# Weights and modulation weights loaded in halves of a unit

## The chip, the cores and the metric

The kernel runs on one core of one Trainium2 chip. The metric is the device time of one execution in microseconds, as a median of runs. TensorE (PE) does the matrix products, VectorE (DVE) and ScalarE (ACT) the elementwise work, GpSimd (POOL) a few fills, and SyncE (SP) issues the DMAs.

## The reference

One sequence of 256 tokens with 1024 channels goes through seven stages in fp32. Before each of the first four stages the input is normalised and modulated by a shift and a scale, and the result is gated; these factors come from a condition vector of 1024 numbers:

```
mod = silu(c) @ ada_w[layer] + ada_b[layer]   # 1024 -> 6*1024, two layers
h = rmsnorm(x) * (1 + scale) + shift
x = x + gate * rmsnorm(mixer(h));  x = x + gate2 * rmsnorm(mlp(h2))
```

The stages are a mixer of a state space scan and neighbourhood attention (mixer0), an MLP of 4096 (mlp0), a chunked mLSTM (mixer1), a second MLP (mlp1), a mixer of three branches (mixer2: softmax attention with a forget gate, a diagonal state space, a gated linear recurrence), a cross attention on 256 memory tokens (cross), and a gated feed-forward of 2816 (ffn). All weights, 214 units of 1 MB, and 48 MB of modulation weights are read from DRAM once.

## The kernel before, in words

The tokens stand transposed in SBUF as a high and a low part (`xh`, `xl`), rounded values and remainders; a weight is split in the same way, and a product is three matmuls (high by high, high by low, low by high).

A **unit** is 1 MB of weights, 128 partitions by 2048 numbers, contiguous in DRAM (`prepare` packs them so). `unit` (line 433) takes a raw buffer of 8 KB a partition out of the pool `raw` (`RAW_BUFS = 3`), issues one DMA on SP (line 440), and then works by halves of 1024 columns: ScalarE writes the rounded high part `wh` (line 450, instruction at L353), VectorE the remainder `wl` (line 451, L362). The cast halves have pools of their own, `wh` and `wl`, with `W_BUFS = 4` buffers each, so two units. In phases that have room some units go to further buffers (`fwh`, `fwl`; `extra`). The users of units are `proj_tok` and `proj_feat` (a projection of 256 outputs: 48 matmuls of 256 columns; both of its output parts run over all eight 128-row slices, so the first half of the unit is needed until three quarters of it, the second to the end), `proj_half`, and `down` (24 matmuls of 512 columns).

The **modulation weights** use the same raw buffers. `first_norm` (line 610) loads the eight units for the first shift and scale at the start (`load`, line 632); VectorE reduces each half against the condition row in one instruction (L640). `ada` (line 732) does the rest in the background of mixer0, mlp0, mixer1 and mlp1, one unit a step: one DMA (line 749) and two VectorE instructions (L753 for shift and scale, L358 and L365 for gates).

The order of the work is not written by hand. The program is traced in the order of the code; `tick` interleaves side work and background steps with the projections by credits. A planner then gives each engine its instructions by priority (the order of the trace) with its own estimates of time, and lets an instruction take a buffer when it expects it to be free. Casts are raised by `CAST_FIRST = 120` places, but `held` keeps them behind the end of the norm between two stages. On the chip each engine runs its list in order; a DMA on SP that waits for its buffer holds all later DMAs, since every load and store of the kernel is issued there.

Of the kernel before, what the change touches and what calls it, by code (L numbers as in the profile page):

```python
# [11 lines left out]
F32 = mybir.dt.float32  # L12
# [7 lines left out]
P = 128  # L20
D = 1024
T = 256
NEG = -1.0e30
NOSYNC = mybir.DependencyInfo(mybir.DependencyClass.NoSync, mybir.DependencyReason.DATA)
RAW_BUFS = 3
W_BUFS = 4
NB_BUFS = 4

CAST_FIRST = 120
# [94 lines left out]
def prepare(i):  # L124
# [40 lines left out]
    for l in range(2):  # L165
        for ch in range(6):
            part = aw[l, :, ch] if ch % 3 == 2 else aw[l, :, ch].T
            ada.append(part.reshape(4, 2, P, D).transpose(0, 2, 1, 3).reshape(4, P, 2048))
    ada = np.concatenate(ada, 0)

    sm = np.zeros((P, N_WSM), f)
# [84 lines left out]
    for gg in range(2):  # L256
        blk[gg, :, :, :, gg, :] = c5[:, :, gg].transpose(3, 0, 1, 2)
    c5 = blk.reshape(P, 2 * 16 * 32)
    return {
        "x": i["x"][0], "mem": i["mem_2"][0], "wts": wts, "ada": ada, "wsm": sm, "cols": cols,  # L260
        "rows": rows, "cst": cst, "hgm": hgm, "tvec": tvec, "nab": nab.reshape(16, P, 512),
        "b5": b5, "c5": c5,
# [8 lines left out]
class Stack:  # L271
    def __init__(self, ctx, tc, aps):
        self.tc, self.nc, self.a = tc, tc.nc, aps
        pool = lambda name, bufs, **kw: ctx.enter_context(tc.tile_pool(name=name, bufs=bufs, **kw))
        self.const = pool("const", 1)
        self.raw_p = pool("raw", RAW_BUFS)
        self.wh_p = pool("wh", W_BUFS)
        self.wl_p = pool("wl", W_BUFS)
        self.xT_p = pool("xT", 1)
# [150 lines left out]
            self.tick(1)  # L430


    def unit(self, u, n, extra=False):
        if self.early > 0:
            extra, self.early = True, self.early - 1
        free = False
        if not extra and self.free > 0:
            free, self.free = True, self.free - 1
        raw = self.raw_p.tile([P, 2048], F32, tag="raw", name="raw")
        self.nc.sync.dma_start(out=raw, in_=self.a["wts"][u])  # L440
        hi, lo = [], []
        for i in range(2):
            src = raw[:, i * 1024:(i + 1) * 1024]
            if extra:
                h, l = self.pt("fwh", [P, 1024], F32R, 4), self.pt("fwl", [P, 1024], F32R, 4)
            else:
                h = self.wh_p.tile([P, 1024], F32R, tag="wh", name="wh")
                l = self.wl_p.tile([P, 1024], F32R, tag="wl", name="wl")
            with self.held(not extra and not free), self.tc.high_priority(CAST_FIRST):
                self.act(h, src)  # L450
                self.tt(l, src, h, ALU.subtract)
            hi.append(h.rearrange("p (k n) -> p k n", n=n))
            lo.append(l.rearrange("p (k n) -> p k n", n=n))
        m = 1024 // n
        return [(hi[k // m][:, k % m], lo[k // m][:, k % m]) for k in range(2048 // n)]
# [154 lines left out]
    def first_norm(self):  # L610


        nc = self.nc
        self.mod[0] = self.const.tile([P, 2, 2, 8], F32, tag="mod0", name="mod0")
        mod = self.mod[0][:, 0]
        self.xh, self.xl = self.new_xT()
        tps = []

        def transposed():
            tps.extend(self.ax((P, 2, T)) for _ in range(4))  # L620
            for t in range(2):
                xn = self.xn([P, D])
                r = self.rms(self.x[t], xn)
                for g in range(2):
                    gs = slice(g * 512, (g + 1) * 512)
                    self.act(xn[:, gs], self.x[t][:, gs], scale=r[:, 0:1])
                    for k in range(4 * g, 4 * g + 4):
                        self.transpose(tps[k // 2][:, k % 2, t * P:(t + 1) * P], xn[:, k * P:(k + 1) * P])

        sums = []  # L630

        def load(u):
            s8 = self.sm(4, "fns", bufs=4)
            sums.append(s8)
            for what in range(2):
                raw = self.raw_p.tile([P, 2048], F32, tag="raw", name="raw")
                nc.sync.dma_start(out=raw, in_=self.a["ada"][what * 4 + u])
                acc = self.pt("acc", [P, D])
                for k in range(2):
                    nc.vector.tensor_tensor_reduce(out=acc, in0=raw[:, k * D:(k + 1) * D], in1=self.crow, scale=1.0, scalar=0.0,  # L640
                                                   op0=ALU.mult, op1=ALU.add, accum_out=s8[:, 2 * what + k:2 * what + k + 1])

        load(0)
        yield
        transposed()
        for u in range(4):
            us = slice(2 * u, 2 * u + 2)
            s8 = sums[u]
            bcol = lambda what: self.col("adab", what * 8 + 2 * u, 2)
            self.tt(mod[:, 1, us], s8[:, 0:2], bcol(0), ALU.add)  # L650
            self.tt(s8[:, 2:4], s8[:, 2:4], bcol(1), ALU.add)
            self.stt(mod[:, 0, us], s8[:, 2:4], 1.0, self.col("ng", 2 * u, 2), ALU.add, ALU.mult)
            f = self.pt("bp", [P, 2, T], bufs=2)
            for k in range(2):
                kk = 2 * u + k
                a1, b1 = mod[:, 0, kk:kk + 1], mod[:, 1, kk:kk + 1]
                self.act(f[:, k], tps[u][:, k], AF.Identity, scale=a1, bias=b1)
            self.act(self.xh[:, us], f)
            self.tt(self.xl[:, us], f, self.xh[:, us], ALU.subtract)
            if u < 3:  # L660
                load(u + 1)
            yield
# [69 lines left out]
    def ada(self, layer, chunks, G=None, kind="ax"):  # L732

        nc = self.nc
        if self.mod[layer] is None:
            self.mod[layer] = self.const.tile([P, 2, 2, 8], F32, tag=f"mod{layer}", name=f"mod{layer}")
        mod = self.mod[layer]
        for ch in chunks:
            half, what = ch // 3, ch % 3
            acc = self.pt("acc", [P, D])  # L740
            s8 = self.sm(8, "ads")
            rows = []
            for i in range(4 if what == 2 else 0):
                cs = slice(i // 2 * 512, (i // 2 + 1) * 512)
                rows.append(self.pt("grow", [P, 512], F32, 2))
                nc.sync.dma_start(out=rows[-1], in_=self.a["rows"][4 * (i % 2) + layer * 2 + half, cs].partition_broadcast(P))
            for u in range(4):
                raw = self.raw_p.tile([P, 2048], F32, tag="raw", name="raw")
                nc.sync.dma_start(out=raw, in_=self.a["ada"][(layer * 6 + ch) * 4 + u])
                for k in range(2):  # L750
                    w, j = raw[:, k * D:(k + 1) * D], 2 * u + k
                    if what != 2:
                        nc.vector.tensor_tensor_reduce(out=acc, in0=w, in1=self.crow, scale=1.0, scalar=0.0,  # L753
                                                       op0=ALU.mult, op1=ALU.add, accum_out=s8[:, j:j + 1])
                    elif j == 0:
                        self.ts(acc, w, self.cond[:, 0:1], None, ALU.mult)
                    else:
                        self.stt(acc, w, self.cond[:, j:j + 1], acc, ALU.mult, ALU.add)
                yield
            if what == 2:  # L760
                for c in range(2):
                    cs = slice(c * 512, (c + 1) * 512)
                    pb = self.ps(kind)
                    self.matmul(pb, self.ones[:, 0:P], acc[:, cs])
                    self.tt(G[:, cs], pb, rows[2 * c], ALU.add)
                    self.tt(G[:, cs], G[:, cs], rows[2 * c + 1], ALU.mult)
            else:
                bcol = self.col("adab", (layer * 4 + half * 2 + what) * 8, 8)
                if what == 0:
                    self.tt(mod[:, half, 1], s8, bcol, ALU.add)  # L770
                else:
                    self.tt(s8, s8, bcol, ALU.add)
                    self.stt(mod[:, half, 0], s8, 1.0, self.col("ng", (layer * 2 + half) * 8, 8),
                             ALU.add, ALU.mult)
            yield
# [1191 lines left out]
```

## Time and profile before

| | us |
|---|---|
| median of 3 runs | 1510.37 (1508.34 to 1513.8) |
| the profiled execution | 1509.47 |
| its span, first to last instruction | 1507.7 |
| PE busy in it | 1429.2 |
| VectorE busy | 1156.5 |
| ScalarE busy | 864.2 |

The profiled execution has a granted TensorE clock of 0.992 of full speed in the mean. The span is what the rows below are measured in; 1.8 us lie around it. A busy PE is one with a matmul under way: matmuls overlap, so a single one lasts longer than the distance to the next. A wait names who waited and who ended it; a wait of an engine that is not the slowest costs nothing by itself.

### The profile page before, as it was taken

What the parts mean: (1) busy time and instruction counts of PE and PEld (TensorE: products, weight loads), DVE (VectorE), ACT (ScalarE), POOL (GpSimd) and SP (SyncE); (2) the same over time, 40 slices, a digit from 0 to 9 for tenths busy, and PEclk for the clock granted to TensorE, in tenths of its full rate; (3) what the DMA queues carried; (4) which work ended last, traced back from release to release, by engine and by line L of the source; (5) the groups of instructions that cost most, each with busy time, mean ns of one, the idle gap of its engine ahead of it and who ended that gap; (6) DMA issues with size and microseconds to landing.
All of it is one profiled execution on the core that took longest, in us unless ns stands there. A gap on an engine that the chain in (4) does not pass through costs nothing.

```text
span 1507.7 us, 25356 instructions
## 1 busy us (share of the span) xinstructions
PE 1429.2 (95%) x9932; PEld 1299.5 (86%) x9932; DVE 1156.5 (77%) x2201; ACT 864.2 (57%) x1530; POOL 4.5 (0%) x24
## 2 busy tenths in 40 slices
PE   2998899999999999999999999999999899999999
PEld 2987787898988889998888998988889888799998
DVE  7788989876778987666989868689997886565555
ACT  4686675654555655554657756467546357454443
POOL 0000000000000000000000000000000000000000
PEclk9999999999999999999999999999999999999999
DMA  9665787587877686444586665554444264245552
GB/s 345 243 183 158 275 311 254 195 289 280 318 300 270 233 274 223 156 159 163 192 326 225 237 206 193 189 188 149 155 168 140 96 254 154 84 168 173 191 189 92
DMA packets 63226, 316.53 MB, mean 210 GB/s; under 512 B 6521, under 2 KB 16385, under 8 KB 29314
## 3 DMA queue, kind: packets, MB, share of 16 engines
q1 hardware_dynamic: 63106, 314.90, 59.1%
q8 instruction: 78, 1.28, 0.3%
q14 instruction: 42, 0.34, 0.1%
HBM read 305.82 MB, written 9.06 MB: 209 GB/s over the span
## 4 chain that ended last, share of the span: by engine, by line
PE 71%; DVE 16%; DMA 6%; ACT 5%; issue 2%; SPq 0%; ACTq 0%; DVEq 0%
PE mm L368 48%; PE ax L368 21%; DVE wl L362 4%; DMA bp<-cs_d 2%; DMA raw<-in_wts 2%; PE ax L372 2%; ACT wh L353 2%; ACT xn L353 1%; DVE merged L362 1%; DVE acc L753 1%; DVE acc L640 1%; DVE s5w L362 1%; DVE s5w L375 1%; DMA meml<-mem_d 0%; DMA grow<-in_rows 0%
## 5 line engine op out<-in xcount | busy, mean ns | idle before, releaser
L362 DVE TENSOR_TENSOR wl<-raw,wh 128x1024 fp32r<-128x1024 f32 x400 | 483.9, 1222 | 197.0 <-ACT wh L353 194.0
L353 ACT ACTIVATE wh<-raw 128x1024 fp32r<-128x1024 f32 x400 | 417.7, 1056 | 342.6 <-PE mm L368 213.3
L368 PE MATMUL mm<-xh,wh 128*128 128x256 f32 x1536 | 443.5, 289 | 10.2 <-ACT wh L353 7.3
L368 PE MATMUL mm<-xh,wl 128*128 128x256 f32 x1536 | 440.7, 287 | 4.3 <-DVE wl L362 4.2
L368 PE MATMUL mm<-xl,wh 128*128 128x256 f32 x1536 | 439.9, 286 | 0.0
L368 PEld LDWEIGHTS mm<-xh,wh 128*128 128x128 f32 x1536 | 298.7, 194 | 17.7 <-ACT wh L353 9.1
L368 PEld LDWEIGHTS mm<-xh,wl 128*128 128x128 f32 x1536 | 298.4, 194 | 8.6 <-DVE wl L362 5.8
L368 PEld LDWEIGHTS mm<-xl,wh 128*128 128x128 f32 x1536 | 298.7, 194 | 3.6 <-issue 1.8
L368 PE MATMUL mm<-wh,xh 128*128 128x256 f32 x496 | 143.4, 289 | 0.0
L368 PE MATMUL mm<-wl,xh 128*128 128x256 f32 x496 | 141.5, 285 | 0.0
L368 PE MATMUL mm<-wh,xl 128*128 128x256 f32 x496 | 141.2, 285 | 0.0
L368 PE MATMUL ax<-wh,mhh 128*128 128x512 f32 x256 | 102.4, 400 | 0.0
L368 PE MATMUL ax<-wl,mhh 128*128 128x512 f32 x256 | 101.3, 396 | 0.0
L368 PE MATMUL ax<-wh,mhl 128*128 128x512 f32 x256 | 101.3, 396 | 0.0
L368 PEld LDWEIGHTS mm<-wh,xh 128*128 128x128 f32 x496 | 95.2, 192 | 2.2 <-issue 1.8
L368 PEld LDWEIGHTS mm<-wl,xh 128*128 128x128 f32 x496 | 95.3, 192 | 1.9 <-issue 1.5
L368 PEld LDWEIGHTS mm<-wh,xl 128*128 128x128 f32 x496 | 95.3, 192 | 0.4 <-issue 0.3
L368 PEld LDWEIGHTS ax<-wh,mhl 128*128 128x128 f32 x256 | 48.1, 188 | 12.0 <-DVE mhl L362 0.4
L368 PEld LDWEIGHTS ax<-wh,mhh 128*128 128x128 f32 x256 | 48.2, 188 | 10.7 <-ACT wh L353 0.5
L368 PEld LDWEIGHTS ax<-wl,mhh 128*128 128x128 f32 x256 | 48.1, 188 | 10.6 <-issue 0.2
L753 DVE CUSTOM_DVE_ANT_0 acc<-raw,crow 128x1024 f32<-128x1024 f32 x32 | 39.0, 1219 | 5.0 <-DMA raw<-in_ada 4.8
L365 DVE SCALAR_TENSOR_TENSOR acc<-raw,cond,acc 128x1024 f32<-128x1024 f32 x28 | 35.9, 1281 | 8.5 <-DMA raw<-in_ada 8.4
(488 smaller groups left out, 2503.0 us busy)
## 6 DMA issues: line engine op xcount, KB each, us to landing
raw<-in_wts SPq DMA_DIRECT2D x214, 1024.0 KB, 4.9
raw<-in_ada SPq DMA_DIRECT2D x48, 1024.0 KB, 5.9
nb<-in_nab SPq DMA_DIRECT2D x16, 256.0 KB, 5.3
grow<-in_rows SPq DMA_DIRECT2D x16, 256.0 KB, 5.5
bp<-cs_d SPq DMA_DIRECT2D x16, 256.0 KB, 5.8
s5tab<-s5t SPq DMA_DIRECT2D x16, 256.0 KB, 2.2
s5tl<-s5tab SPq DMA_DIRECT2D x16, 256.0 KB, 2.9
meml<-mem_d SPq DMA_DIRECT2D x2, 1024.0 KB, 7.5
```

What stands on the lines that cost most here:

```text
L353: return self.nc.scalar.activation(out=out, in_=in_, func=func, **kw)
L362: return self.nc.vector.tensor_tensor(out=out, in0=in0, in1=in1, op=op)
L365: return self.nc.vector.scalar_tensor_tensor(out=out, in0=in0, scalar=s, in1=in1, op0=op0, op1=op1)
L368: return self.nc.tensor.matmul(out, lhsT, rhs, start=start, stop=stop)
L372: return self.nc.tensor.transpose(out, in_, self.ident[0:k, 0:k])
L375: return self.nc.vector.tensor_tensor_scan(out=out, data0=d0, data1=d1, initial=init, op0=op0, op1=op1)
L640: nc.vector.tensor_tensor_reduce(out=acc, in0=raw[:, k * D:(k + 1) * D], in1=self.crow, scale=1.0, scalar=0.0, op0=ALU.mult, op1=ALU.add, ...
L753: nc.vector.tensor_tensor_reduce(out=acc, in0=w, in1=self.crow, scale=1.0, scalar=0.0, op0=ALU.mult, op1=ALU.add, accum_out=s8[:, j:j + 1])
```

## The change

A raw buffer becomes a half, 128 by 1024 numbers (4 KB a partition), and there are four of them. A new helper `raw` takes one and issues its DMA of 512 KB; in DRAM each partition's piece is then 4 KB out of a row of 8 KB. `unit` calls it twice, once ahead of each half's cast. `first_norm` and `ada` call it ahead of each reduction. The cast pools go from four to five halves each. What is computed stays the same.

```diff
--- before.py
+++ after.py
@@ -22,8 +22,8 @@
 T = 256
 NEG = -1.0e30
 NOSYNC = mybir.DependencyInfo(mybir.DependencyClass.NoSync, mybir.DependencyReason.DATA)
-RAW_BUFS = 3
-W_BUFS = 4
+RAW_BUFS = 4
+W_BUFS = 5
 NB_BUFS = 4
 
 CAST_FIRST = 120
@@ -430,17 +430,20 @@
             self.tick(1)
 
 
+    def raw(self, unit, i):
+        raw = self.raw_p.tile([P, 1024], F32, tag="raw", name="raw")
+        self.nc.sync.dma_start(out=raw, in_=unit[:, i * 1024:(i + 1) * 1024])
+        return raw
+
     def unit(self, u, n, extra=False):
         if self.early > 0:
             extra, self.early = True, self.early - 1
         free = False
         if not extra and self.free > 0:
             free, self.free = True, self.free - 1
-        raw = self.raw_p.tile([P, 2048], F32, tag="raw", name="raw")
-        self.nc.sync.dma_start(out=raw, in_=self.a["wts"][u])
         hi, lo = [], []
         for i in range(2):
-            src = raw[:, i * 1024:(i + 1) * 1024]
+            src = self.raw(self.a["wts"][u], i)
             if extra:
                 h, l = self.pt("fwh", [P, 1024], F32R, 4), self.pt("fwl", [P, 1024], F32R, 4)
             else:
@@ -633,11 +636,10 @@
             s8 = self.sm(4, "fns", bufs=4)
             sums.append(s8)
             for what in range(2):
-                raw = self.raw_p.tile([P, 2048], F32, tag="raw", name="raw")
-                nc.sync.dma_start(out=raw, in_=self.a["ada"][what * 4 + u])
                 acc = self.pt("acc", [P, D])
                 for k in range(2):
-                    nc.vector.tensor_tensor_reduce(out=acc, in0=raw[:, k * D:(k + 1) * D], in1=self.crow, scale=1.0, scalar=0.0,
+                    w = self.raw(self.a["ada"][what * 4 + u], k)
+                    nc.vector.tensor_tensor_reduce(out=acc, in0=w, in1=self.crow, scale=1.0, scalar=0.0,
                                                    op0=ALU.mult, op1=ALU.add, accum_out=s8[:, 2 * what + k:2 * what + k + 1])
 
         load(0)
@@ -745,10 +747,8 @@
                 rows.append(self.pt("grow", [P, 512], F32, 2))
                 nc.sync.dma_start(out=rows[-1], in_=self.a["rows"][4 * (i % 2) + layer * 2 + half, cs].partition_broadcast(P))
             for u in range(4):
-                raw = self.raw_p.tile([P, 2048], F32, tag="raw", name="raw")
-                nc.sync.dma_start(out=raw, in_=self.a["ada"][(layer * 6 + ch) * 4 + u])
                 for k in range(2):
-                    w, j = raw[:, k * D:(k + 1) * D], 2 * u + k
+                    w, j = self.raw(self.a["ada"][(layer * 6 + ch) * 4 + u], k), 2 * u + k
                     if what != 2:
                         nc.vector.tensor_tensor_reduce(out=acc, in0=w, in1=self.crow, scale=1.0, scalar=0.0,
                                                        op0=ALU.mult, op1=ALU.add, accum_out=s8[:, j:j + 1])
```

## Rows read from the trace of the kernel before

**Rows 1.** Busy time, share and instructions of each engine over the whole span, page.
```profile
PE 1429.2 (95%) x9932; PEld 1299.5 (86%) x9932; DVE 1156.5 (77%) x2201; ACT 864.2 (57%) x1530; POOL 4.5 (0%) x24
```

**Rows 2.** Waits of PE over the span: who for whom, us, times, longest.
```profile
PE ax L372 <- ACT xn L353: 16.1, 1, 16.1
PE mm L368 <- ACT nf L353: 8.7, 1, 8.7
PE mm L368 <- ACT wh L353: 7.3, 3, 3.9
PE mm L368 <- DVE wl L362: 4.8, 6, 2.2
```

**Rows 3.** Stretches: length, busy time per engine, granted clock, DMA share, GB/s.
```profile
0.00:37.00 37.00, 8.43 (x36) 7.28 (x37) 29.11 (x75) 18.36 (x34) 0.68 (x10) 1.00 0.90 343
144.90:148.30 3.40, 3.40 (x15) 2.35 (x14) 3.40 (x6) 1.60 (x3) 0.00 (x0) 0.50 0.26 55
179.00:186.00 7.00, 5.67 (x25) 5.38 (x26) 7.00 (x19) 4.22 (x5) 0.00 (x0) 0.51 0.93 337
300.00:450.00 150.00, 150.00 (x970) 135.85 (x971) 110.20 (x135) 77.88 (x106) 0.00 (x0) 1.00 0.80 292
1350.00:1500.00 150.00, 150.00 (x1043) 139.86 (x1042) 84.91 (x107) 66.53 (x87) 0.00 (x0) 1.00 0.47 164
```

**Rows 4.** Chain of work in order of time: start us, us, what.
```profile
376.12 5.74 PE mm L368 x48
381.86 5.60 PE ax L368 x24
```

**Rows 5.** Timelines around three stalls: start us, us, engine, operation, [idle before <- releaser].
```profile
141.62 0.69 ACT L353 ACTIVATE xn<-bp,ccol 128x128 f32<-128x128 f32 x2 [2.74 <-DMA bp<-cs_d]
...
143.31 0.38 PE L368 MATMUL mm<-xh,wh 128*128 128x256 f32 x1 [2.27 <-ACT wh L353]
...
171.48 1.76 SPq L440 DMA_DIRECT2D raw<-in_wts  x1
...
178.69 2.00 ACT L353 ACTIVATE wh<-raw 128x1024 fp32r<-128x1024 f32 x2 [2.05 <-DMA raw<-in_wts]
...
179.80 0.58 PE L368 MATMUL mm<-xh,wh 128*128 128x256 f32 x1 [3.88 <-ACT wh L353]
...
181.12 0.58 PE L368 MATMUL mm<-xh,wl 128*128 128x256 f32 x1 [0.53 <-DVE wl L362]
...
1120.84 0.39 PE L368 MATMUL mm<-xh,wl 128*128 128x256 f32 x1 [2.20 <-DVE wl L362]
```

**Rows 6.** Instructions that touch the raw tile: ns min/median/max, first and last start.
```profile
L353 ACT ACTIVATE wh<-raw x400: 1038/1060/1067, 21.3 to 1492.8; 128x1024 fp32r<-128x1024 f32 x134
...
L362 DVE TENSOR_TENSOR wl<-raw,wh x400: 1198/1224/1229, 24.2 to 1493.9; 128x1024 fp32r<-128x1024 f32 x134
...
L440 SPq DMA_DIRECT2D raw<-in_wts x214: 327/328/1765, 13.6 to 1478.0; - x107
...
L753 DVE CUSTOM_DVE_ANT_0 acc<-raw,crow x32: 1203/1218/1227, 361.3 to 571.3; 128x1024 f32<-128x1024 f32 x32
```

**Rows 7.** DMA issues of the span: engine, count, KB each, median us to landing.
```profile
raw<-in_wts SPq DMA_DIRECT2D x214, 1024.0 KB, 4.9
...
crow<-crow_d SPq DMA_DIRECT2D x2, 512.0 KB, 3.3
```

**Rows 8.** The same for loads issued in 300 to 460 us.
```profile
raw<-in_wts SPq DMA_DIRECT2D x28, 1024.0 KB, 5.8
raw<-in_ada SPq DMA_DIRECT2D x16, 1024.0 KB, 5.6
```

**Rows 9.** Waits of ScalarE in 300 to 460 us, and of SP over the span.
```profile
ACT wh L353 <- DMA raw<-in_wts: 33.4, 9, 6.2
...
ACT wh L353 <- PE mm L368: 26.3, 18, 3.1
...
SPq L440 <- DVE wl L362: 463.5, 96, 21.2
```

## The prediction

> **What bounds the kernel now.** I read the page's busy times first: TensorE (PE) has matmuls in flight for 1429.2 of 1507.7 us, VectorE 1156.5, ScalarE 864.2 [rows 1]. So at most 78.5 us are there to be won by feeding PE better, and the first 37 us, with PE busy for 8.43, hold 28.6 of them [rows 1, 3]. The list of PE's waits comes next: the two longest, 16.1 and 8.7 us, belong to the first norm at the start; for cast weights PE waited only 7.3 us (high part, three times) and 4.8 us (low part, six times) [rows 2]. The reader is to see that weights are nearly always ready. The stretches show where nothing can be won: in 300 to 450 us (first MLP) and 1350 to 1500 us (the last feed-forward) PE is busy without a break at full clock [rows 3]. There a projection unit takes 5.74 us (48 matmuls) and a down unit 5.60 us (24) in the chain [rows 4]; that is the pace at which a unit has to be loaded and cast.
>
> Three places are left where PE stands for weights: 2.27 us at 143.31, 3.88 and 0.53 us at 179.80 and 181.12, and 2.20 us at 1120.84, 8.88 us together [rows 5]. Each is followed by a stretch at half the granted clock, the lower of the two levels (1.2 for 2.4 GHz): 0.50 over 3.4 us after the first, 0.51 over 7.0 us around the second, and again 0.50 over 3.4 us after the third, whose row is like the first one's; PE loses 1.7, 3.4 and 1.7 us of full-speed work in them, 6.8 together [rows 3]. All that the change can give back in the middle of the kernel is so 8.88 + 6.8 = 15.7 us.
>
> **The change part by part.**
> Memory: three units raw at 8 KB a partition plus two times four cast halves at 4 KB were 24 + 32 = 56 KB; four raw halves plus two times five cast halves are 16 + 40 = 56 KB. Nothing else has to move.
>
> Depth: before, 3 units raw and 2 cast stand ahead of PE, 5 in all; after, 2 raw and 2.5 cast, 4.5. At 5.7 us a unit that is 28.5 against 25.7 us. The cast store, the part next to PE, gains half a unit, 2.85 us; the raw store loses one unit, 5.7 us.
>
> Issue: 262 loads (214 + 48) become 524. One issue takes SP 328 ns [rows 6], so 262 x 0.328 = 86 us more on SP. I cost it at nothing: SP's largest wait, 463.5 us in 96 pieces, is for the cast that frees a raw buffer [rows 9], so an issue is late by 0.33 us at worst, and only where SP comes late from another wait; what stands behind it (scan rows, biases, tables, norm rows) is late by the same.
>
> Casts and reductions: their shapes and counts stay (1060 ns on ScalarE, 1224 ns on VectorE, 1218 ns for a modulation half [rows 6]); only what they wait for changes. A cast can begin when half a unit has landed. Two 512 KB loads stand in the list of transfers beside the units' 4.9 us: the row that is read back from DRAM takes 3.3 [rows 7]. I take 3.3 us for a lone half, so a cast that waits for its data starts 1.6 us sooner; the bounds are 0 (a half as slow as a unit) and 2.45 (half of 4.9).
>
> The Trainium skill speaks against this edit: "DMA: Bandwidth & Descriptors", section "Bandwidth", tells to batch loads to 1 MiB or more, which a unit is and a half is not, and its table for the software queue falls off below that. Its fit of 2.0 us plus bytes at 436 GB/s would give 3.2 us for a half and 4.4 for a unit, an estimate; the trace has 3.3 and 4.9 [rows 7]. If the loss of rate that it warns of decides, the time is that of the second rival.
>
> The stall at 143.31: PE waits for a cast on ScalarE that stands behind work which itself waited 2.74 us for a broadcast row [rows 5]. One more cast half gives 2.85 us of lead, more than the gap of 2.27; it is the order of casts on ScalarE that has to use it. The stall at 1120.84 is the same on VectorE, a low part behind other vector work, 2.20 us against 2.85. Both go if the planner puts the casts earlier by what the buffer allows. With their slow clock they give 2.27 + 1.7 + 2.20 + 1.7 = 7.9 us.
>
> The stall at 179.80 is another thing: the load was issued at 171.48, its landing ended ScalarE's wait at 178.69, and the first of its casts then held PE until 179.80 [rows 5]. Lead of 2.85 and a landing 1.6 earlier make 4.45 against gaps of 4.41, so on paper it just goes too, for 4.41 + 3.4 = 7.8 us. But it hangs on when SP reaches this load, and a raw store smaller by a unit is reached later. Bounds: 7.8 gained; 5.7 lost, if the whole unit of raw depth is missed. I count 0, between the two.
>
> The first MLP is where the change could cost. Weights and modulation weights come at 292 GB/s [rows 3], so a unit of 1.049 MB every 3.59 us and a half every 1.80. Three unit buffers allow each one a life of 10.8 us, four half buffers 7.2 us. The life before: landing 5.8 us (28 weight units) or 5.6 (16 modulation units) in this stretch [rows 8], then 1.06 + 2 x 1.22 = 3.5 for casting or 2 x 1.22 = 2.4 for reducing; by 28 to 16 that is 8.8 us, which leaves up to 1.9 us of waiting in queues, 0.95 a half. ScalarE waits there 33.4 us for raw data and 26.3 us for PE [rows 9], so the loads are about level with the need. After: landing L, plus 2.28 or 1.22, plus 0.95, is L + 2.85 on average, and 7.2 allow L up to 4.35. A lone half takes 3.3; units are 0.9 slower in this stretch than their median of 4.9, and a half with two others ahead of it I put between 3.8 and 4.4. So it just holds. At the lower end this costs nothing; at L = 4.9 the stage's 150 us stretch by 0.55 / 7.2 = 8%, 11.5 us, less the 2.85 us that the fuller cast store holds: 8.6. At L = 5.8, a half as slow as a unit, it would be 1.45 / 7.2 of 150 less 2.85 = 27 us. I take 1 us, near the lower end, since the lone 512 KB row is the nearest one.
>
> The start: sixteen modulation halves (eight units) are reduced on VectorE, which is busy 29.11 of the first 37 us, with transfers at 0.90 of the DMA engines [rows 3]. Finer loads let a reduction begin up to 1.6 us sooner; a unit less in flight can make a later load wait. I take 0; bounds: 1.6 gained and, one unit's landing once too late, 4.9 lost. Stage borders, where casts are held until the norm is done, keep their first cast: 0.
>
> Sum against the profiled execution (1509.5 us, of which the span is 1507.7): 1509.5 - 7.9 + 1.0 = 1502.6. The median of the runs, 1510.4, is 0.9 above that execution, so as a median 1503.5 us.
>
> **The rivals.**
> First, hidden: the casts are not the only thing in those queues. At 143 and 1120 the work ahead of the cast stays ahead of it, another instruction ends the wait (a scan step, a broadcast row), and the MLPs cannot get faster. For it: PE waits for dozens of small things beside weights, and the norm waits at the start, 16.1 + 8.7 us [rows 2], are untouched. Against it: the gaps named end on a cast. Time: 1510.4 with 1 us either way for the new order, 1509 to 1512.
>
> Second, slower: raw loads run short wherever modulation weights are read as well, first of all in the first MLP. It decides from a half's landing of 4.35 us on. For it: the two stores are already level there [rows 9], and units land 0.9 later than elsewhere. Against it: 3.3 us for a lone 512 KB, and 2.85 us more cast store. Time: 8.6 us at L = 4.9, no gain in the first mixer (same loads), 1509.5 + 8.6 + 0.9 = 1519.
>
> Third, all three stalls go and the MLP holds: 1510.4 - 15.7 = 1494.7. For it: 4.45 us against 4.41 at 179.80. Against: that this is level, and rests on SP's order.
>
> **How the numbers follow.** Less than 0.3% (4.5 us) can't be told from no change here, so faster is below 1505.9 and slower above 1514.9. Forecast (two stalls go, MLP nearly holds) 0.42, with its own range 1498 to 1508; hidden 0.27; slower 0.23; all three 0.08. Faster: 0.36 of the forecast, 0.08 of the third, 0.01 of the first: 0.45. Same: 0.06 + 0.23 + 0.01 of the second: 0.30. Slower: 0.03 of the first (the planner's order for the worse) and 0.22: 0.25. The range goes from 1494, just under the third, to 1521, past the second; under 2 in 10 is left out, mostly landings above 5 us.
>
> **What would show it.** Right: no PE gap over 1 us on a cast near 143 and 1120, and full clock there; half loads that land in under 4.35 us in 300 to 450, with PE still unbroken. Wrong: PE waits on casts inside the first MLP, or ScalarE's wait for raw data well over 33.4 us there; the stall at 179.80 longer than 3.88; new gaps on broadcast rows in the first mixer. If PE's total for weights stays at 7.3 + 4.8 us and the time with it, the first rival was right.

## The result, and the profile after

The changed kernel is slower: 1578.3 us median (1568.7 to 1586.5, 4 runs) against 1510.9; the ratio is 1.0443, 95% interval 1.0381 to 1.0506. The forecast was 1503.5 us, with a range up to 1521. The profiled execution of the changed kernel took 1568.65 us (span 1566.9), the fastest of its four runs; so 59.2 us of span are seen in the traces, against 67.4 us between the medians.

Where the time went, by stage. The table is worked out from the two traces: a stage runs from its first matmul on cast weights to that of the next stage (the first one from the start of the span).

| stage | before, us | after, us | difference | modulation weights loaded there |
|---|---|---|---|---|
| start and mixer0, input part | 234.1 | 245.0 | +10.9 | yes |
| mixer0, output part | 50.0 | 48.9 | -1.1 | no |
| first filler (memory keys), with the norm | 13.8 | 21.3 | +7.5 | no |
| mlp0 | 187.6 | 205.5 | +17.9 | yes, most |
| mixer1, input part | 177.5 | 185.0 | +7.5 | yes |
| mlp1 | 187.0 | 195.1 | +8.1 | yes, little |
| mixer2 | 301.7 | 306.3 | +4.6 | no |
| cross | 68.9 | 70.3 | +1.4 | no |
| ffn | 194.3 | 194.4 | +0.2 | no |

The other four (three fillers, mixer1's output) add 2.2 us. The page's busy times of the changed kernel, the same line as [rows 1]:

```profile
PE 1447.0 (92%) x9932; PEld 1308.2 (83%) x9932; DVE 1157.3 (74%) x2201; ACT 863.2 (55%) x1530; POOL 4.5 (0%) x24
```

The work is the same: PE, VectorE and ScalarE have as many instructions as before. PE's time without a matmul went from 78.5 to 119.9 us, 41.4 of the 59.2. The other 17.8 are longer busy time: the granted clock fell from 0.992 to 0.984 of full speed in the mean, which over the two spans is 13 us of full-speed work (an estimate). Three stretches: the first MLP before, the first MLP after, and a part of the last feed-forward after (columns as in [rows 3]):

```profile
298.00:485.00 187.00, 185.85 (x1168) 166.20 (x1168) 138.43 (x171) 100.94 (x137) 0.00 (x0) 1.00 0.80 292
```
```profile
315.30:520.80 205.50, 190.43 (x1170) 165.97 (x1168) 137.07 (x170) 98.46 (x132) 0.00 (x0) 1.00 0.80 266
...
1400.00:1550.00 150.00, 150.00 (x1072) 141.27 (x1071) 86.04 (x108) 67.83 (x89) 0.00 (x0) 1.00 0.56 179
```

The feed-forward is as unbroken as before; the first MLP, where PE had breaks of 1.2 us in all, now has 15 us of them, and the bytes arrive at 266 in place of 292 GB/s. Who waits there, and for whom (waits and issues of 315 to 521 us, the whole stage; [rows 9] and [rows 8] have 160 us of the 188 before):

```profile
ACT wh L353 <- DMA raw<-in_wts: 78.2, 43, 7.7
...
PE ax L368 <- DVE wl L362: 6.3, 7, 2.7
PE mm L368 <- DVE wl L362: 4.6, 6, 1.4
...
ACT wh L353 <- PE mm L368: 2.7, 2, 1.5
```

```profile
raw<-in_wts SPq DMA_DIRECT2D x65, 512.0 KB, 4.9
raw<-in_ada SPq DMA_DIRECT2D x34, 512.0 KB, 5.5
```

The reader is to see the reversal: ScalarE waited 33.4 us for raw data and 26.3 for PE (33.9 and 26.6 over the whole stage), and now 78.2 and 2.7. The casts are no longer held back by PE; they come as soon as data lands, and that is too late. A half lands in 4.9 or 5.5 us, not in 3.8 to 4.4. One turn of it in the timeline, at 426 us:

```profile
424.87 1.23 DVE L753 CUSTOM_DVE_ANT_0 acc<-raw,crow 128x1024 f32<-128x1024 f32 x1 [3.00 <-DMA raw<-in_ada]
...
426.13 0.33 SPq L435 DMA_DIRECT2D raw<-in_wts  x1
...
427.29 0.50 PE L368 MATMUL ax<-wl,mhh 128*128 128x512 f32 x1 [1.62 <-DVE wl L362]
...
428.01 1.06 ACT L353 ACTIVATE wh<-raw 128x1024 fp32r<-128x1024 f32 x1 [5.33 <-DMA raw<-in_wts]
```

A reduction waits for its modulation half; only its end frees the buffer into which SP loads the next weights (426.13); PE stands for a low part, and ScalarE has been idle for 5.33 us.

### The profile page after: what moved, and what is told of

The parts are those of the page before. It is cut to its first block, busy times and chain, and to the rows that moved or that the text cites. A ratio compares the mean times of both kernels' runs of the same rounds, so it can differ in the third digit from the quotient of the medians.

```text
span 1566.9 us, 26020 instructions
## 1 busy us (share of the span) xinstructions
PE 1447.0 (92%) x9932; PEld 1308.2 (83%) x9932; DVE 1157.3 (74%) x2201; ACT 863.2 (55%) x1530; POOL 4.5 (0%) x24
## 3 DMA queue, kind: packets, MB, share of 16 engines
q1 hardware_dynamic: 100834, 314.92, 62.2%
## 4 chain that ended last, share of the span: by engine, by line
PE 43%; DMA 22%; DVE 22%; ACT 8%; issue 5%; SPq 0%; ACTq 0%; DVEq 0%
PE mm L368 28%; PE ax L368 13%; DMA raw<-in_wts 12%; DVE wl L362 6%; DMA raw<-in_ada 6%; ACT wh L353 3%; DVE merged L362 2%; PE ax L372 1%; ACT xn L353 1%; DMA grow<-in_rows 1%; DVE s5w L375 1%; DVE acc L753 1%; DVE s5w L362 1%; DVE acc L365 1%; DMA bp<-nM_d 1%
```

## The experiments

Three theories: **depth** (the raw store fell from 3 MB to 2, and can't come round fast enough), **granularity** (loads of 512 KB are dear in themselves) and **order** (the planner's lists changed). Times are medians of the runs; ratios are to the kernel before, run on the same chip, with their 95% intervals.

**Six raw halves, four cast halves** (the old memory, only the size of a load changed):
```diff
-RAW_BUFS = 4
-W_BUFS = 5
+RAW_BUFS = 6
+W_BUFS = 4
```


> Halves as in the changed kernel, but six raw halves and four cast halves: the raw bytes (24 KB a partition) and cast buffers of the kernel before, only the size of a load changed. Depth theory (the loss is the raw store that went from 3 MB to 2 MB, so that half loads which land in 4.7 to 5.5 us can't come round fast enough where modulation weights are read too): 1500 to 1515 us, the first MLP back to about 187 us. Granularity theory (512 KB loads are dear in themselves, at least 3.6 us of landing for half the bytes and 9% more engine time a byte): still 1550 us or more, the first MLP over 200 us. Order theory (the planner's new order of the queues): no order by depth, anything from 1500 to 1580.

Measured 1524.6 us, ratio 1.0109 (1.0086 to 1.0133); the first MLP takes 192.5 us. The loss follows neither depth nor granularity alone: the greater part of it is gone with the depth, and 16 us stay.

**Two raw units, five cast halves** (the new memory without halving), in the kernel before: `RAW_BUFS = 2`, `W_BUFS = 5`.

> Loads of a whole unit as in the kernel before, but two raw units and five cast halves: the memory of the changed kernel without the halving. Depth theory: at least as slow as the changed kernel, 1575 to 1640 us, since a unit holds its buffer longer than a half. Granularity theory: 1505 to 1520 us.

Measured 1580.2 us, 1.0466 (1.0439 to 1.0493): as slow as the changed kernel, with unit loads that land in 4.9 us. So a loss of this size comes without any half loads. Its first MLP takes 222.7 us, 17 more than in the changed kernel: at the same raw memory halves are the better choice there.

**Four raw and four cast halves**, in the changed kernel: `W_BUFS = 4`.

> The changed kernel with four cast halves in place of five. Depth theory: what the fifth cast half held back in the stages that are short of raw data comes on top, 1580 to 1600 us. Granularity theory: 1575 to 1590 us. If the fifth half does nothing, 1578.

Measured 1585.9 us, 1.0496 (1.0462 to 1.0530). The fifth cast half seems to be worth 8 us, but the interval overlaps that of the changed kernel (1.0381 to 1.0506). The range expected by depth, 1580 to 1600 us, overlaps the one by granularity, 1575 to 1590, so this run does not decide between them.

**Five raw and four cast halves**: `RAW_BUFS = 5`, `W_BUFS = 4`.

> Halves, five raw and four cast: 20 KB of raw a partition, between 16 and 24. Depth theory: between the four-half and the six-half kernels of this call, about 1535 us. Granularity theory: within 10 us of the four-half kernel.

Measured 1550.6 us, 1.0277 (1.0247 to 1.0306). With four cast halves the series is 1585.9, 1550.6, 1524.6 us for 4, 5, 6 raw halves: 35 and 26 us a half. ScalarE's wait for raw weights over the whole span, in the kernels of six, five and four halves:

```profile
ACT wh L353 <- DMA raw<-in_wts: 27.0, 17, 4.6
```
```profile
ACT wh L353 <- DMA raw<-in_wts: 81.9, 45, 5.0
```
```profile
ACT wh L353 <- DMA raw<-in_wts: 110.9, 62, 5.3
```

Not every stage follows the depth. The same stages as above, from one trace of each kernel with four cast halves:

| stage, us | four raw halves | five | six | kernel before |
|---|---|---|---|---|
| start and mixer0, input part | 244.7 | 240.4 | 234.6 | 234.1 |
| mlp0 | 212.2 | 196.1 | 192.5 | 187.6 |
| mixer1, input part | 187.2 | 181.4 | 175.0 | 177.5 |
| mlp1 | 195.9 | 188.9 | 192.4 | 187.0 |

The first three fall with every half that is added, and mlp1 does not.

**Six raw halves, contiguous in DRAM.** The halves of a unit are stored one after the other:
```diff
+    halves = lambda a: np.ascontiguousarray(a.reshape(-1, P, 2, 1024).transpose(0, 2, 1, 3))
...
-        self.nc.sync.dma_start(out=raw, in_=unit[:, i * 1024:(i + 1) * 1024])
+        self.nc.sync.dma_start(out=raw, in_=unit[i])
```


> Six raw halves and four cast halves (1524.6 us), with the weights packed in DRAM so that a half is one block of 512 KB instead of 4 KB out of each row of 8 KB. Pitch theory (the 62.3% of DMA engine time against 59.1% before comes from reading every other 4 KB): the share falls to 59 or 60%, and the time to 1508 to 1515 us. Packet theory (4 KB packets are dearer whatever the pitch) and order theory: share and time stay, 62% and 1520 to 1530 us.

Measured 1518.6 us, 1.0060 (1.0040 to 1.0080); the intervals of the two layouts just miss each other, so some 6 us of the 16 seem to be the pitch. Every engine has the same list of instructions in both kernels; the first MLP goes from 192.5 to 186.4 us, and half loads with no other issue in the 7 us before land in 3.46 us (median of nine) in place of 3.77 (seven). The DMA share did not fall (62.9%, and 62.3 with the pitch): why the same bytes take more engine time, the layout does not explain.

**Units by two loads**, in the kernel before; buffers are taken and freed by the unit:
```diff
-        self.nc.sync.dma_start(out=raw, in_=self.a["wts"][u])
+        for i_ in range(2):
+            self.nc.sync.dma_start(out=raw[:, i_ * 1024:(i_ + 1) * 1024], in_=self.a["wts"][u][:, i_ * 1024:(i_ + 1) * 1024])
```


> The kernel before, with three raw buffers of a whole unit, each filled by two loads of 512 KB that are issued one after the other; buffers are freed by the unit as before. Granularity theory for the 16 us that six raw halves are still slower (loads of 512 KB cost more each): 1520 us or more, DMA share 62%. Order theory (those 16 us come from the planner's order with half buffers, not from the size of a load): within 5 us of the kernel before, 1504 to 1513.

Measured 1529.8 us, 1.0152 (1.0130 to 1.0174). Loads of 512 KB, two a unit, cost about 20 us at the full depth, with the old way of freeing buffers. The planner's order changed here too.

**No modulation loads in the first MLP**, in the changed kernel and in the one before (a part of the edit, shown for the changed one; the reductions there read the condition row instead, so these two kernels leave out four chunks of the modulation):
```diff
-                    w, j = self.raw(self.a["ada"][(layer * 6 + ch) * 4 + u], k), 2 * u + k
+                    idle = kind == "mm" and (layer, ch) != (1, 5)
+                    w, j = self.crow if idle else self.raw(self.a["ada"][(layer * 6 + ch) * 4 + u], k), 2 * u + k
```


> The changed kernel without the loads of modulation weights in the first MLP: its 32 reductions there read the condition row instead, scaled down (so the modulation factors of those four chunks are not the reference's). Depth theory: what slowed this stage was the raw store shared with modulation weights; without them the first MLP takes 185 to 189 us in place of 205.5, and the whole 18 to 25 us less than the changed kernel. A theory of weight loads alone (halves are too slow even for weights): the stage stays at 200 us or more.

> The kernel before with the same loads left out, as the comparison. Depth theory: the first MLP stays at 186 to 188 us, the whole within 5 us of 1508, since these loads never reached PE there.

One execution each: 1558.7 and 1505.2 us. The first MLP of the changed kernel without these loads, and then of the kernel before:

```profile
319.40:507.20 187.80, 186.79 (x1170) 165.94 (x1168) 135.88 (x170) 100.10 (x134) 0.00 (x0) 1.00 0.63 202
```
```profile
295.60:483.70 188.10, 186.77 (x1171) 166.22 (x1170) 139.15 (x173) 102.62 (x137) 0.00 (x0) 1.00 0.57 202
```

187.8 and 188.1 us: halves are fast enough for weights alone at 202 GB/s. The whole loss of this stage came with the modulation loads. The stages behind and ahead of it, whose loads are unchanged, stay slow in the changed kernel (mixer0's input part 248.6 us, mixer1's 188.2, mlp1 196.1).

**Buffers of their own** for the modulation weights of the first MLP: in the changed kernel two halves, in the one before one unit (one line of each edit):
```diff
+        raw = self.pt("adw", [P, 1024], F32, 2) if own else self.raw_p.tile([P, 1024], F32, tag="raw", name="raw")
...
+                raw = (self.pt("adw", [P, 2048]) if kind == "mm" and (layer, ch) != (1, 5) else
+                       self.raw_p.tile([P, 2048], F32, tag="raw", name="raw"))
```


> The changed kernel, but in the first MLP the modulation halves go to two buffers of their own (this phase has room for them), so that the four raw halves are for weights alone and the bytes stay. Theory of the shared store: the first MLP takes 186 to 190 us instead of 205.5, as it did with those loads left out, the whole 1555 to 1565. Traffic theory (the loads of modulation weights slow the halves by their bytes, whoever holds the buffers): the stage stays at 198 us or more, the whole at 1570 or more.

> The kernel before with one unit buffer of its own for the modulation weights of the first MLP; a version that may beat both. Without these loads the kernel before was at most 3.5 us faster, so 1504 to 1509 us is expected by all theories: PE has no break in this stage to win back.

Measured 1563.1 us, 1.0359 (1.0326 to 1.0393, which just overlaps the interval of the changed kernel), and 1511.8 us, 1.0012 (0.9996 to 1.0027). The first MLP of the changed kernel, with all its bytes:

```profile
316.40:508.30 191.90, 188.97 (x1170) 167.06 (x1168) 136.60 (x171) 99.93 (x135) 0.00 (x0) 0.99 0.83 280
```

191.9 in place of 205.5 us, where 186 to 190 was expected: 13.6 of the 17.9 us lost there come back with two more buffers, at 280 GB/s and with landings no shorter (5.5 us for weights, 6.0 for modulation). So buffers were short, not transfer rate, for these 13.6 us. In the kernel before a buffer more gains nothing that can be told (1504 to 1509 us was expected).

**Unit loads of 4 KB rows**: the kernel before with the contiguous halves of above, one load a unit over both of them; every engine's instructions keep their order.
```diff
+        dma_start(out=raw.rearrange("p (h n) -> p h n", h=2), in_=self.a["wts"][u].rearrange("h p n -> p h n"))
```


> The kernel before with the same order of instructions on every engine and one load a unit, but the weights packed in DRAM so that each partition's 8 KB come as two pieces of 4 KB: the packets of the half loads without their number. For the 16 to 21 us by which six raw halves and units by two loads are slower: packet theory: 1520 us or more and a DMA share of 62%. Theory of the number of loads or of the order: 1506 to 1513 us.

Measured 1507.6 us, 0.9997 (0.9979 to 1.0016), DMA share 59.8%. Pieces of 4 KB cost nothing that can be told here; they are not what half loads pay.

**The order stirred**, in the kernel before: `CAST_FIRST = 140` in place of 120.

> The kernel before with casts raised by 140 places in place of 120, which moves the planner's order about half as far from the old one as units by two loads did, with the same loads and buffers. Order theory for the 16 to 21 us: 5 us or more away from 1508, in the mixers. Theory of the loads: within 4 us of 1508.

Measured 1509.5 us, 1.0021 (1.0006 to 1.0035). This stir moves the time by 2 to 3 us. It changed ScalarE's and VectorE's lists about as much as units by two loads did: 86 and 87% of their instructions are still in the old sequence, against 90 and 88%. That speaks against the order as the cause of the 16 to 20 us, but one stir is one sample.

**The sum.** Six halves in place of three units: +16 us (1524.6 against 1508.3). From six to four, at four cast halves: +61.3 (1585.9 less 1524.6). The fifth cast half: about -8. Together +69. These are steps along one path from the kernel before to the changed one, so that they add up to about its +67.4 proves nothing; what they show is the split. What stays open is inside the 16 us: six seem to be the pitch; the rest is the number of loads or the order that they bring about, which no run here separates for certain, since every kernel with twice the loads also got other lists.

## Why the prediction was wrong, point by point

**The failed step is the landing of a half** in "The first MLP is where the change could cost". The rule there was right: a store of 4 halves at 7.2 us each decides, and from L = 4.35 on it is too small. L was put between 3.8 and 4.4 from a lone 512 KB row of 3.3 us [rows 7], "the nearest one"; it measured 4.9 for weights and 5.5 for modulation weights, 5.1 on average. The row was no weight load at all, but a small vector repeated over the partitions. Lone half loads in the changed kernel (no other issue in the 7 us before, seven of them) land in 3.76 us in the median, where lone units take 4.82 (19 of them): half the bytes save 1.06 us.

The rest of the 4.9 comes with other loads in flight: 99 halves of 5.1 us in 205.5 us make 2.5 out at a time in the mean. It hardly grows with their number (5.2 us behind one other half, 5.2 behind two, 5.6 behind three), so how it comes about is not shown. With L = 5.1 the rule gives 0.75 / 7.2 of 150 us less 2.85, that is 13 us. The 150 us were themselves too few: they are the stretch that was read, and the stage has 187.6; with these the rule gives 16.7. The term that was counted at 1 us measured 17.9. The life of a buffer agrees: by the prediction's terms it is 5.1 + 2.85 = 7.95 us, and by the rate, 4 x 0.524 MB at 266 GB/s, it is 7.9. A buffer so had next to no time to spare, and 7.2 were allowed.

**The second failure is where it was looked for.** The account was made for one stage; "It decides ... wherever modulation weights are read as well" stood in the second rival, but its price counted the first MLP alone; the start stands at 0 and mixer1 has no term. The start and mixer0's input lost 10.9 us and mixer1's input 7.5, and these two follow the depth in the series above, though PE's waits in mixer1 are mostly for other work than weights. The other losses are not shown to be depth. mlp1 lost 8.1 us, yet PE waited there for other work, 4.0 us of it for one step of mixer2's tables and 0.8 for a weight's low part:

```profile
PE mm L372 <- DVE s5bb L1354: 4.0, 1, 4.0
```

It is also slow at the full depth, 192.4 us with six halves and 194.9 with units by two loads. The filler after mixer0, with its norm, lost 7.5 us; it takes 13.8 us before, 13.5 with four raw and four cast halves, 14.3 with two raw units, 15.8 with six halves and 18.8 with five. PE waits there for steps of the norm, probably by the planner's lists, which was not tested. Nor do mixer2's 4.6 us, without modulation loads, have a cause that was tested. The rival also priced waits alone, without the slower clock of the changed kernel. So even its 1519 us was 59 too fast. The direction of that rival was the right one, at 0.23.

**The first MLP's reserve.** The 2.85 us of the fuller cast store were counted as cover. The runs show a fifth cast half worth some 8 us in the whole, not told clear of noise: a store can be late once on it, not for 150 us.

**The stalls.** The cast that held PE at 143.31 is no longer in its way, but PE then waits 1.49 us for other work in the same place, and the slow clock stays; the stall at 1120.84 went from 2.20 to 1.79 us, and a slow stretch still follows, now only behind another 1.49 us that PE waits for a scan at 1175.67; the one at 179.80, counted at 0, stayed at 3.44 and 0.53 us. PE's rows at the three places, and the stretches behind the first and the third:

```profile
147.16 0.33 PE L372 MATMUL ax<-cst,xs 128*128 128x128 f32 x1 [1.49 <-DVE xs L365]
...
184.21 0.58 PE L368 MATMUL mm<-xh,wh 128*128 128x256 f32 x1 [3.44 <-ACT wh L353]
...
1173.33 0.39 PE L368 MATMUL mm<-xh,wl 128*128 128x256 f32 x1 [1.79 <-DVE wl L362]
```
```profile
148.70:152.10 3.40, 3.40 (x14) 2.57 (x15) 3.09 (x7) 0.94 (x2) 0.00 (x0) 0.50 0.39 86
1176.10:1179.50 3.40, 3.40 (x31) 1.73 (x24) 2.91 (x5) 1.66 (x3) 0.00 (x0) 0.51 0.70 202
```

So of the 7.9 us forecast from two stalls 0.78 and 0.41 came: this part of the first rival (another wait takes the place) was right. PE's few waits for weights told what had gone wrong before, not what the buffers were holding off; the waits of ScalarE [rows 9] were level, which is no margin, and they were read as "it just holds".

**What was right.** In ffn the issues on SP cost nothing to be seen: with twice the loads it is the same to 0.2 us. Elsewhere a part of the 16 to 20 us of half loads at full depth may be theirs. That nothing could be won in the MLPs or in ffn held. The first rival (hidden) had its time wrong, and the third failed altogether.

**The page's rule.** The Trainium skill, "DMA: Bandwidth & Descriptors", section "Bandwidth", tells to load 1 MiB or more at a time; it points the right way, and units by two loads agree with it (1.0152). The fit on that page, in section "Anatomy of one DMA — SWDGE (gpsimd) path", is for loads issued from GpSimd; it makes a half 1.2 us shorter than a unit, an estimate, and the lone loads of these traces, issued from SP, give 1.06 us. But the greater part of this loss need not come from small loads: two raw units, loaded by the MiB, are as slow (1.0466).

## What to carry to other kernels

Count a prefetch store as bytes over life: buffers times size, divided by the time from issue to release, is the most that it can deliver, and that has to exceed the need of the hungriest stage by a margin, with all that shares the store. Halving a load does not halve its life (3.76 against 4.82 us alone, about 5 in a queue), so a store can keep its rate when it is cut finer at the same bytes (+16 us here), and loses it when the bytes go as well (+61 more). When the engine that consumes a store waits as long for data as for its own consumer, as ScalarE did here with 33.4 and 26.3 us, there is nothing to take away.

## What the runs showed of the hardware that was not expected

The same 315 MB took 59.1% of the DMA engines' time over the span before and 62.2% of a longer one after, 9% more; with 4 KB pieces in unit loads it is 59.8%, so not the packets but the number of loads, or how they meet, goes with it. And reading every other 4 KB in place of whole blocks cost some 6 us in 1520, close to what can be told, and 0.3 us a lone half (3.77 against 3.46).
